# A two-layer encoder on one core: the identity made on GpSimd, x at the head of ScalarE's DMA ring

## The chip, the cores and the metric

The kernel runs on one core of a Trainium2 chip. A core has five engines that run their own instruction queues side by side: TensorE (PE in the profile, with its weight loads as PEld), VectorE (DVE), ScalarE (ACT), GpSimd (POOL) and SyncE (SP). SyncE and ScalarE each issue DMA transfers into a ring of their own; sixteen DMA engines serve both. The metric is the device time of one execution in microseconds, the median of several runs. The kernel before took 605.46 us (604.07 to 605.92 in 3 runs).

## The reference

Two layers over one sequence of 256 tokens, width 1024. Each layer has a mixer with three kinds of attention heads beside each other, and a gated feed-forward part with a short convolution over the tokens:

```python
def mixer_sublayer(x, n1, w_in_l, qg, kg, rpb_l, og, w_out_l, tables):
    h = rms_norm(x, n1)
    proj = h @ w_in_l                       # 1024 -> 2560, cut into q, k, v of three groups
    ...
    out_a = neighbourhood_attention(qa, ka, heads(va, H_NA), rpb_l, na_idx, na_dr, na_dc)
    out_d = dilated_window_attention(qd, kd, heads(vd, H_DIL), dil_idx, dil_val)
    out_c = gqa_block_attention(qc, kc, heads(vc, H_GKV))
    mix = jnp.concatenate([rms_norm(out_a, og[:NA_W]), rms_norm(out_d, ...), rms_norm(out_c, ...)], axis=-1)
    return x + mix @ w_out_l

def channel_sublayer(x, n2, w_gu, cw, cb, w_dn):
    h = rms_norm(x, n2)
    g, u = jnp.split(h @ w_gu, 2, axis=-1)
    g = depthwise_conv_centred(g, cw, cb)
    return x + (jax.nn.gelu(g, approximate=False) * u) @ w_dn
```

For the opening only the first two lines matter: the norm of x and its product with `w_in`.

## The kernel before

**Numbers in two parts.** All large products are done in fp32r, with each operand cut into a high and a low part, and three products per tile: high by high, high by low, low by high (`mm3`). The weights come as raw fp32 in units of up to 1 MB, in four buffers (`wp_raw`); `split` casts each 128x384 or 128x512 piece to the high part on ScalarE (CAST `wp_hi`) and subtracts on VectorE for the low part (TENSOR_TENSOR `wp_lo`).

**The opening.** x is kept on chip as `xs` (`const_x` in the profile): two tiles of 128 tokens by 1024 columns, read as eight column blocks of 128. Its transpose is wanted for the first product. For each block, two 128x128 transposes go through TensorE with the identity `ident` as the moving side (`psw_w<-const_ident,const_x`); ScalarE then scales the result by the norm weight and rounds it to the high part (ACTIVATE `act_hT`), and VectorE makes the low part (SCALAR_TENSOR_TENSOR `act_hT`). This is `split_T`. The norm weights themselves arrive as 16 rows of 128 and are transposed with the same identity (`gains_T`, `psw_w<-const_ident,act_s2k`) before the first ACTIVATE can scale with them. The sums of squares for the norm (`mean_squares`, ACTIVATE `act_s2k<-const_x`, 128x512) run on ScalarE in between; their result enters only later, as a factor on rows.

The first projection, `dq`, is 384 wide: its weights are unit 0 (k blocks 0 to 3, loaded in four pieces) and unit 1 (k blocks 4 to 7, in two). Each unit gives 24 products of 128x384, for two tiles of tokens, four k blocks and three parts.

**Warm-ups.** Before any data is there, TensorE runs products of a constant tile (`const_warm`, filled by GpSimd) into a buffer that nobody reads: `WARM` of them at once, and `WARM_MORE` at a low priority, which the planner puts into holes.

**What sets the order.** Nothing is issued as the Python code runs. `Plan` records every operation with its inputs and outputs, estimates a duration (`cost`), and `Plan.order` then simulates the engines and picks, each time, the operation that can start first; ties go to the lower rank. Rank is the operation's number in the record plus `later` shifts plus an entry of `PLACES`, a long table of small corrections by operation number. `LANDS` tells the planner when each of the first loads is to be expected, in ns. Each engine then runs its list strictly in that order, so an instruction that waits holds up all that stands behind it on its engine.

The first loads stand in a list of their own, `START`: which queue issues what, in which order. `("act", "x", (0, 1))` means that ScalarE's queue loads one block of x, the 0th; "w" is a piece of unit 0, "g" a group of norm weights, "ident" the identity from a constant in memory. These loads are emitted ahead of every other DMA. Eight completion semaphores are used in turn, so the ninth transfer can be issued only when the first has landed, and so on.

Of the kernel before, what the change touches and what calls it, by code (L numbers as in the profile page):

```python
# [18 lines left out]
P = 128  # L19
# [28 lines left out]


START = [  # L50
    ("act", "g", 0), ("sync", "w", 0), ("act", "ident", 0), ("act", "x", (0, 1)), ("sync", "w", 1),
    ("sync", "x", (1, 1)), ("sync", "x", (2, 2)), ("sync", "w", 2), ("sync", "w", 3), ("sync", "x", (4, 2)),
    ("sync", "x", (6, 2)), ("sync", "g", 1), ("sync", "g", 2),
]


LANDS = (3000, 3700, 3200, 3800, 4700, 5000, 6000, 6700, 7300, 8300, 9300, 9350, 9400)


WARM, WARM_MORE, WARM_W = 13, 6, 256  # L60

SUM_ACT, SCALE_ACT = ("dq", "dk", "cq"), ("dk",)

# [166 lines left out]
def handover(a, b):  # L230
# [1 line left out]


PLACES = {
# [35 lines left out]
}  # L270


# [244 lines left out]
def cost(engine, method, args, kw, ins):  # L517

    out = args[0]
    if method == "dma_start":  # L520
        w = out if isinstance(out, View) else args[1]
        small = min(out.shape[-1], args[1].shape[-1]) < 128
        spread = isinstance(args[1], bass.AP) and args[1].ap[0][0] == 0
        stored = isinstance(out, View) and out.tile.pool.dram
        size = 4 * math.prod(w.shape) * (2 if small or spread else 1.5 if stored else 1)
        return 620 if engine == "POOL" else 480, 0, size, None
    n = out.width()
    psum = any(v.tile.pool.psum for v in ins)
    if engine == "PE":
        if method == "transpose":  # L530
            return n / 2.25 + 2.5, 0, 0, "turn"
        n = args[2].width()
        ns = {512: 231.6, 384: 174.5, 256: 118.0}.get(n, n / 2.25 + 2.5)
        if args[1].dtype == mybir.dt.bfloat16:
            ns = 213.0
        if args[1].width() < P:
            return 216.0, 0, 0, "side"
        return ns, 0, 0, "half" if args[1].shape[0] < P else "full"
    if engine == "ACT":
        extra = 88 * sum(isinstance(kw.get(k), View) for k in ("scale", "bias")) + 92 * ("accum_out" in kw)  # L540
        ns = 0.833 * n + (53 if psum else 95) + extra
        return ns, ns + (15 if "accum_out" in kw else 105), 0, None
    if engine == "DVE":
        if method in ("reduce_sum", "reduce_max"):
            n = args[1].width()
        ns = 1.04 * n + (126 if method == "scalar_tensor_tensor" else 68)
        return ns, ns + 82, 0, None
    if method == "memset":
        ns = 190 + 0.83 * n
    elif method == "tensor_copy":  # L550
        ns = 0.92 * n + 100
    elif kw.get("op") == ALU.pow:
        ns = 560 + 150 * n
    elif method == "tensor_scalar":
        ns = 350 + 3.8 * n
    else:
        ns = 830 if out.width() == S else 350 + 3.1 * n
    return ns, ns - 95, 0, None
# [3 lines left out]
def encoder_kernel(  # L562
# [57 lines left out]

    warm = const.tile([P, P], mybir.dt.bfloat16, tag="warm", name="warm")
    nc.gpsimd.memset(warm, 1.0)
    wps = psa.tile([P, WARM_W], F32, tag="a", name="wps")

    def warmed(n):
# [59 lines left out]
    def load(i):  # L685
# [13 lines left out]
        if i == 0:  # L699
            for by, what, c in START:  # L700
                by = nc.scalar if by == "act" else nc.sync
                if what == "w":
                    by.dma_start(rv[:, c], v[:, c])
                elif what == "x":
                    load_x(*c, by)
                elif what == "ident":
                    by.dma_start(ident, c_ident)
                elif what == "g":
                    by.dma_start(gl0 if c == 0 else gl1[16 * c - 16 : 16 * c], gsrc[c])
            nc.first_loads = len(nc.ops)  # L710
        else:
            for c in range(0, a, 2 if i == 1 else a):
                e = c + 2 if i == 1 else a
                nc.sync.dma_start(rv[:, c:e], v[:, c:e])
# [870 lines left out]
```

## Time and profile before

| | |
|---|---|
| median of 3 runs | 605.46 us (604.07 to 605.92) |
| the profiled execution | 605.0 us |
| its span | 603.0 us |
| PE busy | 595.2 us (99%) |
| ScalarE, VectorE, GpSimd busy | 413.3, 471.1, 78.0 us |
| DMA | 121.43 MB, mean 201 GB/s |

The span counts from the first to the last instruction on the core; the 2.0 us around it belong to the execution. The busy time of TensorE includes matmuls whose ends are modelled, so two that overlap in the pipeline show longer than their spacing. In timelines, a name such as `psa_a<-wp_hi,act_hT` is the tile written and the tiles read, without buffer numbers. Nearly all instructions carry one source line, L514, since the planner emits them there; so groups are told apart by tiles and shapes.

### The profile page before, as it was taken

The numbers are of one execution on the slowest core, as the hardware profiler recorded it, in microseconds if no ns is written. First come the engines' busy times: TensorE is split into PE (matmuls) and PEld (weight loads), VectorE is DVE, ScalarE is ACT, GpSimd is POOL, SyncE is SP. The second block draws the span as 40 slices with busy tenths as digits, with TensorE's granted clock in tenths as the row PEclk, the third lists the DMA queues.
The fourth block names the chain that finished last, engine by engine and source line by source line (L and its number), as shares of the span: only waits on it lengthen the run. The fifth ranks groups of instructions, "written<-read, shape, count | busy, mean of one in ns | idle before, by whom it ended". The sixth has DMA issues, their size and how long they took to land.

```text
span 603.0 us, 9676 instructions
## 1 busy us (share of the span) xinstructions
PE 595.2 (99%) x3423; PEld 511.5 (85%) x3423; DVE 471.1 (78%) x983; ACT 413.3 (69%) x1035; POOL 78.0 (13%) x124
## 2 busy tenths in 40 slices
PE   7999999999999999999999999999999999999997
PEld 6998787788888888888899988778888888888886
DVE  2788989897779797987977897668976677767875
ACT  4798989586575685756777898676765555646651
POOL 0652140160000000000014213421000000000000
PEclk9999999999999999999999999999999999999999
DMA  8896323555679898988635826944465455745511
GB/s 276 264 230 193 106 88 109 193 186 181 225 222 281 255 365 298 345 312 275 218 107 173 277 74 245 304 154 139 147 203 174 165 161 199 254 164 193 162 65 71
DMA packets 85216, 121.43 MB, mean 201 GB/s; under 512 B 9880, under 2 KB 69880, under 8 KB 85168
## 3 DMA queue, kind: packets, MB, share of 16 engines
q1 hardware_dynamic: 82992, 112.22, 57.2%
q0 software_dynamic: 1728, 8.39, 4.0%
q8 instruction: 27, 0.44, 0.3%
q10 hardware_dynamic: 448, 0.20, 0.1%
q14 instruction: 21, 0.17, 0.1%
HBM read 110.93 MB, written 9.88 MB: 200 GB/s over the span
## 4 chain that ended last, share of the span: by engine, by line
PE 92%; DMA 3%; DVE 2%; ACT 1%; issue 0%; POOL 0%; ACTq 0%; SPq 0%; DVEq 0%
PE psw_w L514 50%; PE psa_a L514 42%; DMA act_nab<-dram_scr 2%; DMA const_x<-in_x_dram 1%; DMA dram_scr<-act_nab 1%; DVE wp_lo L514 1%; ACT act_s2k L514 0%; DVE act_z L514 0%; DVE act_nab L514 0%; POOL small_rstd L514 0%; ACT wp_hi L514 0%; DVE act_sw L514 0%; ACT act_hT L514 0%; ACTq L514 0%; DVE act_s2k L514 0%
## 5 line engine op out<-in xcount | busy, mean ns | idle before, releaser
L514 DVE TENSOR_TENSOR wp_lo<-wp_raw,wp_hi 128x512 fp32r<-128x512 f32 (+2 forms) x332 | 233.8, 736 | 34.8 <-ACT wp_hi L514 19.3
L514 ACT CAST wp_hi<-wp_raw 128x512 fp32r<-128x512 f32 (+2 forms) x332 | 202.3, 666 | 19.0 <-PE psw_w L514 10.8
L514 PE MATMUL psw_w<-act_hT,wp_hi 128*128 128x512 f32 x704 | 182.8, 393 | 0.0
L514 PEld LDWEIGHTS psw_w<-act_hT,wp_hi 128*128 128x128 f32 x704 | 128.3, 188 | 23.9
L514 PE MATMUL psa_a<-wp_hi,act_hT 128*128 128x384 f32 (+2 forms) x448 | 114.6, 336 | 0.6 <-ACT wp_hi L514 0.6
L514 PEld LDWEIGHTS psw_w<-act_hT,wp_lo 128*128 128x128 f32 x704 | 100.2, 190 | 8.2
L514 PE MATMUL psw_w<-act_hT,wp_lo 128*128 128x256 f32 x704 | 105.2, 282 | 0.0
L514 PEld LDWEIGHTS psa_a<-wp_hi,act_hT 128*128 128x128 f32 x448 | 79.4, 191 | 3.8 <-ACT wp_hi L514 0.7
L514 PE MATMUL psa_a<-wp_lo,act_hT 128*128 128x384 f32 (+2 forms) x224 | 75.3, 338 | 0.0
L514 ACT COPY act_s2k<-psw_w 128x256 f32<-128x256 f32 x88 | 31.7, 372 | 57.5 <-PE psw_w L514 57.1
L514 DVE TENSOR_TENSOR act_s2k<-psw_w,act_s2k 128x256 f32<-128x256 f32 x88 | 36.1, 421 | 42.4 <-ACT act_s2k L514 41.9
L514 PE MATMUL psa_a<-wp_lo,act_ch 128*128 128x512 f32 (+1 forms) x176 | 68.6, 392 | 0.0
L514 PE MATMUL psa_a<-wp_hi,act_cl 128*128 128x512 f32 (+1 forms) x176 | 67.9, 392 | 0.0
L514 PE MATMUL psa_a<-wp_hi,act_ch 128*128 128x512 f32 (+1 forms) x176 | 65.9, 393 | 0.0
L514 PEld LDWEIGHTS psa_a<-wp_lo,act_hT 128*128 128x128 f32 x224 | 42.8, 191 | 2.3 <-DVE wp_lo L514 1.0
L514 PEld LDWEIGHTS psa_a<-wp_hi,act_cl 128*128 128x128 f32 x176 | 33.0, 188 | 7.0
L514 PEld LDWEIGHTS psa_a<-wp_lo,act_ch 128*128 128x128 f32 x176 | 32.9, 188 | 6.6
L514 PEld LDWEIGHTS psa_a<-wp_hi,act_ch 128*128 128x128 f32 x176 | 32.9, 188 | 6.6
L514 DVE SCALAR_TENSOR_TENSOR act_s2k<-act_s2k,act_cw,act_s2k 128x255 f32<-128x255 f32 x88 | 37.1, 478 | 0.0
L514 ACT ACTIVATE act_s2k<-act_s2k 128x512 f32<-128x512 f32 x22 | 13.9, 632 | 31.4 <-DVE act_s2k L514 31.4
L514 ACT ACTIVATE act_s2k<-act_s2k,act_cw 128x256 f32<-128x256 f32 x44 | 24.1, 596 | 14.9 <-DVE act_s2k L514 14.8
L514 POOL TENSOR_TENSOR small_rstd<-small_ms,const_mh 128x6 f32<-128x6 f32 (+2 forms) x26 | 31.3, 1204 | 15.8 <-DVE small_ms L514 14.1
(129 smaller groups left out, 710.7 us busy)
## 6 DMA issues: line engine op xcount, KB each, us to landing
wp_raw<-in_w_gate_up_dram SPq DMA_DIRECT2D x44, 1024.0 KB, 5.2
wp_raw<-in_w_down_dram SPq DMA_DIRECT2D x22, 1024.0 KB, 5.4
wp_raw<-in_w_in_dram SPq DMA_DIRECT2D x14, 768.0 KB, 4.6
wp_raw<-in_w_in_dram SPq DMA_DIRECT2D x8, 1024.0 KB, 5.4
wp_raw<-in_w_out_dram SPq DMA_DIRECT2D x8, 768.0 KB, 6.5
dram_khi<-act_mixT_hi SPq DMA_DIRECT2D x4, 768.0 KB, 5.0
dram_klo<-act_mixT_lo SPq DMA_DIRECT2D x4, 768.0 KB, 8.3
wp_lo<-dram_klo POOLq DMA_DIRECT2D x4, 768.0 KB, 5.7
```

The source lines that it names most:

```text
L514: getattr(o.engine.real, o.method)(*map(real, o.args), **{k: real(v) for k, v in o.kw.items()})
```

## The change

Four things are edited.

1. The identity is no longer loaded. GpSimd fills it with zeros and writes ones where row and column are equal, right behind the fill of the warm-up tile.
2. The list of first loads: ScalarE's ring now carries block 0 and block 1 of x, and nothing else. The norm weights move to second place on SyncE's ring, behind the first weight piece; block 1 of x leaves that ring.
3. `LANDS` follows the new list, `WARM` goes from 13 to 14, and `cost` knows the new GpSimd operation.
4. `PLACES` is a new table, since operation numbers move.

```diff
 START = [
-    ("act", "g", 0), ("sync", "w", 0), ("act", "ident", 0), ("act", "x", (0, 1)), ("sync", "w", 1),
-    ("sync", "x", (1, 1)), ("sync", "x", (2, 2)), ("sync", "w", 2), ("sync", "w", 3), ("sync", "x", (4, 2)),
-    ("sync", "x", (6, 2)), ("sync", "g", 1), ("sync", "g", 2),
+    ("act", "x", (0, 1)), ("sync", "w", 0), ("act", "x", (1, 1)), ("sync", "g", 0), ("sync", "w", 1),
+    ("sync", "x", (2, 2)), ("sync", "w", 2), ("sync", "w", 3), ("sync", "x", (4, 2)), ("sync", "x", (6, 2)),
+    ("sync", "g", 1), ("sync", "g", 2),
 ]
-LANDS = (3000, 3700, 3200, 3800, 4700, 5000, 6000, 6700, 7300, 8300, 9300, 9350, 9400)
-WARM, WARM_MORE, WARM_W = 13, 6, 256
+LANDS = (3400, 3500, 4000, 3600, 5000, 6000, 6800, 7400, 8100, 8900, 8950, 9000)
+WARM, WARM_MORE, WARM_W = 14, 6, 256
...
 PLACES = {
-    76: -86, 77: -11, 80: -43, 82: -43, 112: -35, 123: 210, 150: 217, 155: -22, 156: -22, 159: -329, 174: 52,
+    40: 94, 60: -9, 127: -3, 129: -5, 151: 348, 161: -236, 180: 82, 191: -272, 193: 107, 195: 81, 236: 39, 258: -19,
...
     if method == "memset":
         ns = 190 + 0.83 * n
+    elif method == "affine_select":
+        ns = 900
...
     nc.gpsimd.memset(warm, 1.0)
+    nc.gpsimd.memset(ident, 0.0)
+    nc.gpsimd.affine_select(ident, ident, [[-1, P]], ALU.not_equal, 1.0, base=0, channel_multiplier=1)
...
                 elif what == "x":
                     load_x(*c, by)
-                elif what == "ident":
-                    by.dma_start(ident, c_ident)
```

ScalarE's queue at the start of the program, before (`act_s2k_79` are the norm weights, `const_x` is x, `psw_w` the transposed x in PSUM):

```order
L514 DMA act_s2k_79<-in_norm_g_dram 16x128
L514 DMA const_ident_88<-in_c_ident_dram 128x128
L514 DMA const_x_93<-in_x_dram 128x2x128
L514 ACT_TABLE_LOAD
L514 CAST wp_hi_113<-wp_raw_81 128x384
L514 ACTIVATE act_hT_127<-psw_w_118,const_gains_116 128x256
L514 CAST wp_hi_113<-wp_raw_81 128x384
L514 ACTIVATE act_hT_127<-psw_w_133,const_gains_116 128x256
L514 ACTIVATE act_s2k_150,small_ssx_149<-const_x_93 128x512
L514 ACTIVATE act_s2k_160,small_ssx_149<-const_x_93 128x512
```

And now:

```order
L511 DMA const_x_79<-in_x_dram 128x2x128 x2
L511 ACT_TABLE_LOAD
L511 CAST wp_hi_113<-wp_raw_81 128x384
L511 ACTIVATE act_hT_133<-psw_w_119,const_gains_130 128x256
L511 ACTIVATE act_hT_133<-psw_w_124,const_gains_130 128x256
L511 CAST wp_hi_113<-wp_raw_81 128x384
L511 ACTIVATE act_s2k_154,small_ssx_153<-const_x_79 128x512
L511 ACTIVATE act_s2k_163,small_ssx_153<-const_x_79 128x512
```

Two blocks of x head the queue, and the second hT piece stands ahead of the second cast.

TensorE's queue before, from the last of the 13 first warm-ups on (of the warm-ups only the matmul rows' first and the places between are shown; `act_s2k_79` are the norm weights):

```order
L514 MATMUL psw_w_109<-const_ident_88,act_s2k_79 128x16
L514 LDWEIGHTS const_warm_77
L514 MATMUL psa_a_83<-const_warm_77 128x256
...
L514 MATMUL psw_w_118<-const_ident_88,const_x_93 128x128 x2
...
L514 MATMUL psw_w_133<-const_ident_88,const_x_93 128x128 x2
L514 MATMUL psa_a_139<-wp_hi_113,act_hT_127 128x384
```

And now, behind 15 warm-ups:

```order
L511 MATMUL psw_w_116<-const_ident_85,act_s2k_89 128x16
L511 MATMUL psw_w_119<-const_ident_85,const_x_79 128x128 x2
L511 MATMUL psw_w_124<-const_ident_85,const_x_79 128x128 x2
L511 LDWEIGHTS const_warm_77
L511 MATMUL psa_a_83<-const_warm_77 128x256
...
L511 MATMUL psa_a_143<-wp_hi_113,act_hT_133 128x384
```

Before, two warm-ups stood between the norm weights' transpose and the first of x, and four between the first and second pair of x. Now the three transposes follow each other, and five warm-ups stand between them and the first product.

GpSimd's queue now (before, the fill of `const_mh` followed that of `const_warm` directly, and there was no `const_ident`):

```order
L511 MEMSET const_warm_77 128x128
L511 MEMSET const_ident_85 128x128
L511 ISA
L511 AFFINE_SELECT const_ident_85<-const_ident_85 128x128
L511 MEMSET const_mh_101 128x32
L511 TENSOR_TENSOR small_s1x_230<-small_ssx_153 128x2
```

The ISA row is a configuration of the engine that stood before `small_s1x` and now stands before the select.

65 rows, old and new, of the table PLACES are left out of this document.

## The prediction

> **What bounds the kernel now.** I read the busy times first, then the same in stages, then TensorE's waits, then the opening in order of time. The first line of the page names the engine:
>
> ```profile
> PE 595.2 (99%) x3423; PEld 511.5 (85%) x3423; DVE 471.1 (78%) x983; ACT 413.3 (69%) x1035; POOL 78.0 (13%) x124
> ```
>
> TensorE (PE) has work in 595.2 of 603.0 us. A share over the whole run hides where the other 7.8 us lie, so the next view cuts the span (columns: stretch, its length, then busy time of PE, weight loads, DVE, ACT, POOL, granted clock, DMA share, GB/s):
>
> ```profile
> 0.00:7.00 7.00, 3.80 (x17) 2.15 (x17) 0.65 (x2) 1.79 (x2) 0.46 (x6) 1.00 0.61 181
> 7.00:17.00 10.00, 9.43 (x46) 8.64 (x46) 5.14 (x13) 7.38 (x21) 0.30 (x2) 1.00 1.01 347
> 17.00:100.00 83.00, 82.51 (x564) 72.72 (x566) 72.36 (x205) 72.85 (x258) 30.85 (x45) 1.00 0.54 160
> 100.00:300.00 200.00, 200.00 (x1071) 169.87 (x1068) 167.35 (x291) 134.03 (x258) 14.03 (x25) 1.00 0.78 256
> 300.00:590.00 290.00, 290.00 (x1682) 250.19 (x1681) 218.90 (x465) 195.65 (x498) 32.34 (x47) 1.00 0.53 176
> ```
>
> From 17 to 590 us TensorE lacks half a microsecond. So whatever brings the start of that dense stretch forward brings the end forward by as much, and a change in the opening is worth exactly the shift of the first product of the second weight unit (unit 1). In the timeline of the opening that product is the last row here (start, duration, engine, operation, tiles, count, idle time before and its releaser):
>
> ```profile
> 0.98 2.95 PE L514 MATMUL psa_a<-const_warm 128*128 128x256 bf16 x13 [0.98 <-POOL const_mh L514]
> 4.24 0.26 PE L514 MATMUL psw_w<-const_ident,act_s2k 16*128 16x16 f32 x1 [0.30 <-DMA const_ident<-in_c_ident_dram]
> 6.95 0.69 PE L514 MATMUL psw_w<-const_ident,const_x 128*128 128x128 f32 x2 [1.92 <-DMA const_x<-in_x_dram]
> 7.43 1.06 PE L514 MATMUL psa_a<-const_warm 128*128 128x256 bf16 x4
> 9.36 0.84 PE L514 MATMUL psa_a<-wp_hi,act_hT 128*128 128x384 f32 x2
> 12.75 0.34 PE L514 MATMUL psa_a<-wp_lo,act_hT 128*128 128x384 f32 x1
> 15.21 0.68 PE L514 MATMUL psa_a<-wp_hi,act_hT 128*128 128x384 f32 x3
> 16.98 0.62 PE L514 MATMUL psa_a<-wp_hi,act_hT 128*128 128x384 f32 x2 [0.57 <-ACT wp_hi L514]
> ```
>
> Three things stand there. x arrives only at 6.95: the 13 warm-ups and the gains transpose are long done. Second, a 128x384 product takes 0.52 us at 9.36 (two in 0.84, so 0.32 from start to start), but 0.34 at 12.75 and three in 0.68 at 15.21 (0.17 each): the array runs at half speed up to 12.7. The granted clock in the windows (1.00) doesn't show it; the spacing does. Third, unit 1 waits at the end for ScalarE (ACT), not for data. ScalarE's rows of the same stretch:
>
> ```profile
> 3.43 0.51 ACT L514 CAST wp_hi<-wp_raw 128x384 fp32r<-128x384 f32 x1
> 7.68 0.47 ACT L514 ACTIVATE act_hT<-psw_w,const_gains 128x256 fp32r<-128x256 f32 x1 [3.73 <-PE psw_w L514]
> 8.05 0.50 ACT L514 CAST wp_hi<-wp_raw 128x384 fp32r<-128x384 f32 x1
> 8.96 0.48 ACT L514 ACTIVATE act_hT<-psw_w,const_gains 128x256 fp32r<-128x256 f32 x1 [0.41 <-PE psw_w L514]
> 9.33 0.62 ACT L514 ACTIVATE act_s2k<-const_x 128x512 f32<-128x512 f32 x1
> 13.74 0.84 ACT L514 ACTIVATE act_hT<-psw_w,const_gains 128x256 fp32r<-128x256 f32 x2 [1.54 <-PE psw_w L514]
> 16.41 0.93 ACT L514 CAST wp_hi<-wp_raw 128x384 fp32r<-128x384 f32 x2
> ```
>
> From the first hT at 7.68 to the first cast of unit 1 at 16.41 are 8.73 us, with 0.41 and 1.54 of waiting for TensorE's slow transposes: 6.78 us of ScalarE's own work, eight hT pieces, three casts, four sums of squares.
>
> **The change part by part.** *x.* How long x takes now, and the nearest rows (issue to landing in us, last number; the first row is from the chain of waits, with start and length):
>
> ```profile
> 1.64 5.26 DMA const_x<-in_x_dram
> wp_raw<-in_w_in_dram SPq DMA_DIRECT2D x2, 192.0 KB, 2.8
> const_x<-in_x_dram SPq DMA_DIRECT2D x1, 128.0 KB, 5.1
> const_x<-in_x_dram SPq DMA_DIRECT2D x1, 256.0 KB, 5.6
> 9.42 0.46 SPq L514 DMA_DIRECT2D const_rot<-in_c_rot_dram  x1
> 10.10 0.35 SPq L514 DMA_DIRECT2D const_gq<-in_q_norm_g_dram  x1
> ```
>
> Block 0 is third in its ring now and lands at 6.9. The weight pieces at the head of SyncE's ring need at most 2.8. At the head of ScalarE's ring, issued at 0.72, block 0 lands between 3.5 (2.8) and 6.0 (5.26); I take 3.6, since its rank now is that of the weights. Block 1 follows about 0.45 later (1.17): between 4.0 and 6.4; I take 4.6, since it comes behind twice the bytes. Blocks 2 and 3 keep their slot on SyncE (issued about 2.1, landing now 7.7): at most 7.7, at least 6.3 if all before them flows like the weights; I take 7.2, the old time less 64 KB of identity that is no longer fetched and a part of the slow stretch (181 GB/s up to 7 us, 347 after). The later blocks keep their slots too: SyncE's issues of rot and gq wait for the two x transfers of blocks 4 to 7, which so landed by 9.4 and 10.1; I take 9.2 for the first.
>
> *The identity.* ScalarE's transfer of 64 KB and its issue (0.44 us) go; GpSimd gets a memset and a select over 128x128. Its rows:
>
> ```profile
> 0.72 0.20 POOL L514 MEMSET const_warm<- 128x128 bf16 x1 [0.29 <-POOLq L1570]
> L514 POOL TENSOR_TENSOR act_ccq<-const_rot,const_gq 128x128 f32<-128x128 f32 x2 | 1.5, 766 | 0.1
> L514 POOL TENSOR_TENSOR small_rstd<-small_ms,const_mh 128x8 f32<-128x8 f32 x4 | 6.6, 1644 | 0.3
> ```
>
> The memset ends near 1.1. The trace has no select: its cost lies between the memset's 0.20 and the dearest GpSimd instruction, 1.64; I take 0.77, the pass over the same 128x128. The identity is there at 1.9, at the latest 2.8, against 4.2 now. The 15 warm-ups now ahead of the gains transpose hide it: 0.98 + 15 x 0.213 = 4.18 (13 take 2.95 less the 0.2 that the last one drains). Cost: nothing, up to 4.18; past that, each microsecond is a microsecond. minus_half moves behind the select; its first reader comes past 12 us. Nothing else waits on GpSimd's queue there.
>
> *The norm weights* go from ScalarE's ring to second place on SyncE's. Issued at 1.17 like the second weight piece, which needs 2.8, they land at 4.0: under the same warm-ups. They push that second piece one issue back (0.45 us), to about 4.5; it is first needed after two hT pieces. ScalarE issues two transfers, not three, so its table load ends 0.45 earlier; the first cast then waits for the first weight piece, about as now.
>
> *The sum.* Gains transpose 4.18, first x transpose 4.39, first hT 0.73 later as now (6.95 to 7.68): 5.12. hT, hT, cast (0.37 + 0.37 + 0.50) to 6.36. The squares need x to column 511, so 7.2, a wait of 0.84. From there 1.22 (two squares), 0.82 (two casts), 0.83 (two hT) to 10.07, and 2.67 (as 13.74 to 16.41): unit 1's cast at 12.74 against 16.41, its product at 13.3 against 16.98. **3.7 us earlier.** Does TensorE keep up? With the array at full speed, transposes at 7.2 (0.44), seven products (1.21), eight transposes as soon as x lands at 9.2: hT's third pair can start at 9.9, and ScalarE comes for it at 10.07. It does, barely.
>
> So the clock decides too. In this trace the array doubled at 12.7, after 5.7 us of work without a gap since 6.95; the 2.9 us of warm-ups from 0.98 weren't enough before the gap. The new rows run without a gap from 0.98, so by the same 5.7 us it doubles near 6.7, and the sum above holds.
>
> The Trainium skill, "TensorE: Matmul & The Clock Gate", Part 1, says that the gate opens after about 3.4 us of sustained work, judged in a free-running window. By that rule the doubling here comes between 4.4 and 7.8, the sum stays 601.3, and the first rival below would all but fall out; the trace agrees in kind (a gap of 1.9 us, then 5.7).
>
> *After the opening.* Dense work must find its weights. Between 17 and 590 us no wait for weights shows now. Unit 2, issued by 9.3, moves 768 KB, and ScalarE comes for it near 18.1 (fifth cast from 16.41, 0.43 each): a margin of a few us that shrinks by the shift, with SyncE's issue a little earlier too. I cost it at nothing. The rest of the order is drawn anew from a new table, but TensorE's rows there have the same kinds in the same counts and nearly as many changes between transposes and products; I allow 0.5 us either way.
>
> **The rivals.** *The array stays slow through the opening* (a small gap spoils the run of work). For it: 2.9 us of warm-ups failed here. Against it: 5.7 us without a gap did not. Priced from rows at 0.32 and 0.21 per instruction: four products to 7.6, transposes 8.5, seven products 10.7, four of the eight transposes 11.6, third hT pair 11.85 and not 10.07. The gain falls by 1.8 to 1.9.
>
> *x stays late.* The 5.1 to 5.6 of all x transfers may belong to x's short pieces and not to their rank. Block 1 then lands at 1.17 + 5.26 = 6.4; TensorE has a gap again from 4.85, and by the 5.7 us stays slow to 12.1. Transposes 6.4, warm-ups to 7.9, four products 9.2, transposes 10.0, seven products 12.3, eight transposes at full speed, third hT pair 12.9, then 0.84 + 0.61 + 0.72 + 0.61: cast at 15.8. Gain 0.6. Against it: fewer bytes stand ahead. For it: three x transfers of different rank and ring all took 5.1 to 5.6, so it keeps 0.2.
>
> The Trainium skill, "DMA: Bandwidth & Descriptors", "Issuing engines are not separate DMA queues", says that transfers of all issuers share 16 engines and that a second issuer saves only issue time. By it the new ring itself brings nothing, only the rank, and if block 1 shares the engines with all that SyncE issued it would go as in this rival (604.9). The trace doesn't settle it: x's blocks on both rings took about as long (5.26 and 5.1).
>
> *Slower: the identity is late.* Should GpSimd's select be of another kind than its other instructions (a first use that loads code, say), gains, transposes and hT all stand behind it in TensorE's queue. From the identity to unit 1's cast are 12.74 - 4.18 = 8.56 us, so it decides from 16.41 - 8.56 = 7.9 us on, a select of 6.8 us; at 10 us the run is 2 us longer (607). Against it: nothing on GpSimd takes over 1.7, and its first pow shows no such start.
>
> *The shift isn't carried*: weights or the redrawn order give back 2 us or more. Gain 1.7 or less.
>
> **How the numbers follow.** The profiled execution took 605.0 us (span 603.0 and 2.0 around it), 0.46 under the median of 605.46. 605.0 - 3.7 = 601.3, at the median 601.8. Chances: forecast 0.58 (on its own 600.6 to 602.8: x's third transfer at 6.3 or 7.7 gives a gain of 4.6 or 3.2, and 0.5 for the order); slow array 0.11 (603.6); x late 0.20 (604.9); not carried 0.07 (603.8); slower 0.04. The range 600.6 to 604.5 leaves out the slower case, half of the late x and a little below. Within 0.3% (1.8 us) is about what a measurement here can't tell from no change: faster by more takes the forecast, half of the slow array, a third of the late x (where the array doubles early, gain 2.4) and some of the fourth: 0.71. Same 0.25, slower 0.04.
>
> **What would show it.** Right: x's first transpose near 4.4 and no idle row before it; 128x384 products at 0.17 from 6 to 8 us on; ScalarE waiting for x (not for TensorE) once near 6.4; unit 1's first product near 13.3; less than 1 us of idle from there to 590. Wrong: a wait of TensorE for x over 1 us, products at 0.32 past 10 us, a GpSimd select over 3 us, or new waits for raw weights behind 13 us.

## The result, and the profile after

The changed kernel takes 599.57 us (599.48 to 600.55) against 605.29 us (604.07 to 605.92) for the kernel before beside it: a ratio of 0.9912, 95% interval 0.9893 to 0.993. The profiled execution took 599.53 us with a span of 597.4 us (before 605.0 and 603.0), so 5.5 us less where the prediction had 3.7.

The opening came out as worked out. GpSimd's rows in the changed kernel (start, duration, engine, operation):

```profile
0.86 0.20 POOL L511 MEMSET const_ident<- 128x128 f32 x1
1.15 0.29 POOL L511 TENSOR_SCALAR_AFFINE_SELECT const_ident<-const_ident 128x128 f32<-128x128 f32 x1
```

The identity is there at 1.44 us, far ahead of its first use. TensorE's timeline of the opening:

```profile
0.98 3.32 PE L511 MATMUL psa_a<-const_warm 128*128 128x256 bf16 x15 [0.98 <-POOL const_warm L511]
4.32 0.20 PE L511 MATMUL psw_w<-const_ident,act_s2k 16*128 16x16 f32 x1
4.45 0.66 PE L511 MATMUL psw_w<-const_ident,const_x 128*128 128x128 f32 x4
...
7.07 0.66 PE L511 MATMUL psw_w<-const_ident,const_x 128*128 128x128 f32 x4 [0.48 <-DMA const_x<-in_x_dram]
...
7.74 0.33 PE L511 MATMUL psa_a<-wp_lo,act_hT 128*128 128x384 f32 x1
7.91 0.34 PE L511 MATMUL psa_a<-wp_hi,act_hT 128*128 128x384 f32 x1
...
13.14 0.61 PE L511 MATMUL psa_a<-wp_hi,act_hT 128*128 128x384 f32 x2 [0.34 <-ACT wp_hi L511]
```

Four transposes take 0.66 us at 4.45, where two took 0.69 before: the array is at full speed there already, and two products stand 0.17 us apart at 7.74. Unit 1's first product starts at 13.14 (forecast 13.3, before 16.98). Behind the first hT pieces ScalarE waits for x and not for TensorE, as forecast:

```profile
4.93 0.84 ACT L511 ACTIVATE act_hT<-psw_w,const_gains 128x256 fp32r<-128x256 f32 x2 [0.80 <-PE psw_w L511]
7.13 0.63 ACT L511 ACTIVATE act_s2k<-const_x 128x512 f32<-128x512 f32 x1 [0.79 <-DMA const_x<-in_x_dram]
12.56 1.76 ACT L511 CAST wp_hi<-wp_raw 128x384 fp32r<-128x384 f32 x4
```

The windows (stretch, length, busy PE, weight loads, DVE, ACT, POOL, granted clock, DMA share, GB/s):

```profile
0.00:7.00 7.00, 5.59 (x29) 3.65 (x29) 2.08 (x5) 3.15 (x5) 0.90 (x8) 1.00 0.69 185
7.00:17.00 10.00, 9.59 (x54) 8.37 (x55) 6.66 (x15) 8.97 (x31) 1.69 (x4) 1.00 1.05 353
17.00:100.00 83.00, 83.00 (x575) 73.26 (x575) 74.36 (x208) 74.12 (x259) 29.07 (x44) 1.00 0.58 171
```

By these rows TensorE gained 0.49 us of busy time in the third stretch and nothing behind it. That is too little for the missing 1.8. So I lined up the two traces: TensorE's matmuls in order, each counted at its shortest spacing, and the difference of their start times where the same sum of work stands ahead (called the shift below; it resolves about 0.1 us). It is 3.8 us from 14 us of work on, 5.05 at 110, then flat through the whole feed-forward part, and 5.6 behind layer 2's attention, where it grows between some 365 and 410 us. So 1.25 us come in layer 1's attention and 0.6 in layer 2's. The waits of weight loads (PEld), which the prediction left out, show where such time can hide. Before, 17 to 100 us (total, times, longest):

```profile
PEld psw_w L514 <- ACT act_s2k L514: 1.4, 4, 0.6
...
PEld psa_a L514 <- ACT wp_hi L514: 0.7, 1, 0.7
PEld psa_a L514 <- DVE wp_lo L514: 0.7, 2, 0.4
PEld psw_w L514 <- ACT wp_hi L514: 0.6, 2, 0.4
```

After:

```profile
PEld psw_w L511 <- ACT act_s2k L511: 0.7, 3, 0.3
PEld psw_w L511 <- ACT wp_hi L511: 0.4, 1, 0.4
PEld psw_w L511 <- DVE act_s2k L511: 0.4, 1, 0.4
```

All waits of weight loads for another engine there add up to 4.9 us before and 2.2 after. The busy row of PE hides most of them, since a modelled matmul end covers a late weight load. One wait stands out on VectorE, which masks the neighbourhood bias (a table that layer 1's attention adds to its scores). The bias goes through DRAM and back: VectorE copies it, SyncE stores and loads it. Before, and then after:

```profile
31.83 1.23 DVE L514 COPY act_nab<-act_few 28x1984 f32<-28x1984 f32 x1
48.46 1.43 DVE L514 SCALAR_TENSOR_TENSOR act_nab<-act_nab,const_na 128x576 f32<-128x576 f32 x2 [1.71 <-DMA act_nab<-dram_scr]
```

```profile
27.14 1.24 DVE L511 COPY act_nab<-act_few 28x1984 f32<-28x1984 f32 x1
42.80 1.43 DVE L511 SCALAR_TENSOR_TENSOR act_nab<-act_nab,const_na 128x576 f32<-128x576 f32 x2
```

The copy is 4.7 us earlier, not 3.8, and the mask 5.7 us earlier and without a wait. Two theories fit: the redrawn order took waits away, or the earlier start lets such transfers land in time.

### The profile page after: what moved, and what is told of

It is laid out like the page before. It is cut to its first block, busy times and chain, and to the rows that moved or that the text cites. A ratio compares the mean times of both kernels' runs of the same rounds, so it can differ in the third digit from the quotient of the medians.

```text
span 597.4 us, 9676 instructions
## 1 busy us (share of the span) xinstructions
PE 592.0 (99%) x3424; PEld 509.8 (85%) x3424; DVE 471.0 (79%) x983; ACT 412.7 (69%) x1035; POOL 77.1 (13%) x126
## 4 chain that ended last, share of the span: by engine, by line
PE 97%; ACT 1%; DMA 1%; SPq 0%; issue 0%; DVE 0%; ACTq 0%
PE psw_w L511 51%; PE psa_a L511 46%; DMA const_x<-in_x_dram 1%; ACT act_s2k L511 0%; ACT act_hT L511 0%; ACT wp_hi L511 0%; SPq L511 0%; DVE const_x L511 0%; ACTq L511 0%
## 5 line engine op out<-in xcount | busy, mean ns | idle before, releaser
L511 PE MATMUL psa_a<-wp_hi,act_hT 128*128 128x384 f32 (+2 forms) x448 | 112.0, 333 | 0.3 <-ACT wp_hi L511 0.3
L511 PEld LDWEIGHTS psa_a<-wp_hi,act_hT 128*128 128x128 f32 x448 | 77.8, 189 | 3.5 <-DVE act_hT L511 0.5
```

The source lines that it names most:

```text
L511: getattr(o.engine.real, o.method)(*map(real, o.args), **{k: real(v) for k, v in o.kw.items()})
```

## The experiments

To hold everything still but one thing, these kernels (but for the edits named) take the order of all instructions from a list instead of the planner's choice:

```diff
+ORDER = [0, 1, 2, 3, 4, 5, 6,
...
                 for i in r:
+                    if i != ORDER[len(done)]:
+                        continue
                     o = ops[i]
```

With the list that the planner itself had made, the instructions of each engine are the same as without it.

### 1 to 4: the order, and one instruction in it

Run 1 joins the changed kernel's order up to 20 us of its plan with that of before behind it; run 2 is the mirror image (the order of before up to 24 us, that of the change behind it).

> The changed kernel up to 20 us of its plan, and behind that each engine's instructions in the order in which the kernel before has them. The trace of the change gains 3.8 us up to 17 us and 1.8 us more behind it (1.3 by 100 us, 0.6 between 378 and 398 us). If the redrawn order gives these 1.8 us, this run takes about 601.3 us, and TensorE's weight loads wait about 4.9 us between 17 and 100 us as in the kernel before. If the earlier opening itself gives them (because transfers such as the neighbourhood bias now land in time), it takes about 599.5 us and those waits stay near 2.2 us.

> The mirror image: the kernel before up to 24 us of its plan, and behind that the changed kernel's order on each engine. If the redrawn order is worth 1.8 us by itself: about 603.5 us. If it is worth something only behind the earlier opening: 605.3 us or more, with the vector engine still waiting for the neighbourhood bias near 47 us.

Runs 3 and 4 move one instruction: run 3 is run 1 with

```diff
 VectorE:
-TENSOR_TENSOR wp_lo
 COPY act_nab
+TENSOR_TENSOR wp_lo
```

and run 4 is the changed kernel with the reverse of this.

> The first run of this set with one instruction moved: VectorE's copy of the neighbourhood bias stands one weight split earlier, as in the changed kernel. If that copy's place (it starts the round trip through DRAM for which VectorE waited 1.71 us) makes the 0.67 us step at 54 us: 0.6 to 0.7 us less than the first run of this set. If not: the same time as that run.

> The changed kernel with the same copy moved one weight split later on VectorE, as in the kernel before, and nothing else. If the copy's place makes the 0.67 us step: about 600.2 us, with VectorE waiting about 1 us for the neighbourhood bias near 43 us. If the bias has slack in the new order: 599.5 us, and no such wait.

Measured: run 1 602.2 us (601.16 to 602.9), ratio to before 0.9956, interval 0.9939 to 0.9973, which doesn't meet that of the change; run 2 603.23 (600.88 to 604.55), 0.9974, 0.9958 to 0.999; run 3 601.19 (600.26 to 601.64), 0.9938, 0.9922 to 0.9954; run 4 599.92 (599.39 to 600.66). So **the order gives it, not the earlier start**: with the old order behind it the new opening is worth only 2.8 us, and the new order behind the old opening still 1.7. Together these are 4.5 of the 5.7 us (4.8 where the change was timed again, run 13). In run 1 the weight loads' waits for other engines between 17 and 100 us add up to 5.0 us, as before. The old order even gives shift back. In run 1 the shift is 3.3 us after the opening and 2.35 at the end; its VectorE row:

```profile
45.92 1.43 DVE L809 SCALAR_TENSOR_TENSOR act_nab<-act_nab,const_na 128x576 f32<-128x576 f32 x2 [2.48 <-DMA act_nab<-dram_scr]
```

The bias lands 2.5 us earlier than before where the opening is 3.3 earlier, so VectorE waits longer, and TensorE has a hole of 1.25 us at 52. In run 3 the wait is gone:

```profile
27.61 1.24 DVE L809 COPY act_nab<-act_few 28x1984 f32<-28x1984 f32 x1
43.41 1.42 DVE L809 SCALAR_TENSOR_TENSOR act_nab<-act_nab,const_na 128x576 f32<-128x576 f32 x2
```

One instruction moved by one place is worth 1.0 us in the medians here, though the two intervals still overlap; the traces have 1.0 us in layer 1. Run 4 didn't show the 0.6 us in its median (0.35 over the change, and no more than run 13); its trace has a wait of 0.25 us and 0.6 us less shift from layer 1. In run 2 VectorE still waits 1.68 us for the bias, and the profiled execution, at 604.55 the slowest of that kernel, shows only 0.5 us of gain behind the opening. Its 1.7 us stand on the medians alone.

### 5 and 6: the clock by itself

```diff
-WARM, WARM_MORE, WARM_W = 13, 6, 256
+WARM, WARM_MORE, WARM_W = 13, 29, 256
```

in the kernel before (three of the new warm-ups ahead of the gains transpose, twenty behind it), and in the changed kernel

```diff
-WARM, WARM_MORE, WARM_W = 14, 6, 256
+WARM, WARM_MORE, WARM_W = 4, 6, 256
```

> The kernel before with its own order, its own transfers, and 23 more warm-ups: TensorE has work from 0.98 us until x arrives near 6.9 us. Only the array's speed changes, x doesn't. If the doubled clock carries a part of the gain as the prediction's slow-array rival prices it, 128x384 products stand at 0.17 us from 7 us on and unit 1's first product comes 1.8 to 1.9 us earlier (15.1 us): about 603.2 us. If x's time alone makes the opening's gain: no shift, 605.0 us. If the warm-ups are still running when x comes: up to 1 us later than that.

> The changed kernel and its order with 10 warm-ups fewer ahead of the gains transpose: TensorE works from 0.98 to about 2.05 us and then has nothing until 4.3 us; x, identity and norm weights arrive as in the changed kernel. If the array's speed matters, it is still slow when x's blocks come at 4.4 us (128x384 products at 0.32 us up to 8 to 10 us) and unit 1's first product moves from 13.14 to 13.7 to 15.0 us: 600.1 to 601.4 us. If it doesn't, 599.6 us.

In run 5 unit 1's first product is 2.5 us earlier though x comes only 0.15 us earlier, at full speed from the first transposes on:

```profile
6.80 0.41 PE L813 MATMUL psw_w<-const_ident,const_x 128*128 128x128 f32 x2
...
9.72 0.68 PE L813 MATMUL psa_a<-wp_hi,act_hT 128*128 128x384 f32 x3
...
14.48 0.62 PE L813 MATMUL psa_a<-wp_hi,act_hT 128*128 128x384 f32 x2 [0.54 <-ACT wp_hi L813]
```

And in run 6 it is 1.8 us later than in the changed kernel, though x comes at most 0.2 us later:

```profile
4.46 0.25 PE L809 MATMUL psw_w<-const_ident,act_s2k 16*128 16x16 f32 x1 [2.23 <-DMA act_s2k<-in_norm_g_dram]
...
9.40 0.52 PE L809 MATMUL psa_a<-wp_hi,act_hT 128*128 128x384 f32 x1
9.72 0.52 PE L809 MATMUL psa_a<-wp_lo,act_hT 128*128 128x384 f32 x1
...
14.92 0.62 PE L809 MATMUL psa_a<-wp_hi,act_hT 128*128 128x384 f32 x2 [0.56 <-ACT wp_hi L809]
```

So the array's speed is worth about 1.8 to 2.5 us in the opening, against the 3.8 of the change: the prediction's rival had it at 1.8 to 1.9. The medians: run 6 600.97 us (600.46 to 602.19), 1.4 over the change. Run 5 604.89 (602.3 to 605.33): hardly faster than before, although its opening is. Behind it the old order gave back 1.9 us, 0.5 in layer 1 and 1.5 in layer 2. There TensorE waited for kept weights, which were split in layer 1, parked in DRAM (`dram_khi`, `dram_klo`) and loaded back by GpSimd, a third issuer of transfers beside SyncE and ScalarE:

```profile
PE psa_a L813 <- DMA wp_hi<-dram_khi: 1.5, 1, 1.5
```

Run 6 has the new order, and its shift grows from 2.0 to 3.8 behind the opening, by the same 1.8 us as in the changed kernel.

### 7 and 8: the identity and the rings by themselves

Run 7 is the kernel before, its order kept, with

```diff
-    ("act", "g", 0), ("sync", "w", 0), ("act", "ident", 0), ("act", "x", (0, 1)), ("sync", "w", 1),
+    ("act", "g", 0), ("sync", "w", 0), ("act", "x", (0, 1)), ("sync", "w", 1),
...
+    nc.gpsimd.memset(ident, 0.0)
+    nc.gpsimd.affine_select(ident, ident, [[-1, P]], ALU.not_equal, 1.0, base=0, channel_multiplier=1)
```

Run 8 is the changed kernel, its order kept, without the two GpSimd lines and with

```diff
-    ("act", "x", (0, 1)), ("sync", "w", 0), ("act", "x", (1, 1)), ("sync", "g", 0), ("sync", "w", 1),
+    ("act", "x", (0, 1)), ("sync", "w", 0), ("act", "x", (1, 1)), ("act", "ident", 0), ("sync", "g", 0), ("sync", "w", 1),
```

> The kernel before with its own order, and only the identity changed: GpSimd makes it, ScalarE's transfer of it goes, so that x's block 0 stands second in ScalarE's ring and is issued 0.45 us earlier. If x's lateness belongs to its rank: block 0 comes 0.5 to 0.9 us earlier, but block 1 on SyncE's ring stays where it was (6.7 us), and the array stays slow up to 12 us: a shift of 0 to 0.5 us, 604.5 to 605.0 us. If the identity's 64 KB were what delayed x, both blocks come 1 us or more earlier: 603 to 604 us.

> The changed kernel, its rings and its order, but the identity is loaded, third in ScalarE's ring behind both first x blocks (issued near 1.6 us). From the kernel before, where the identity took 2.9 us from its issue, it lands near 4.6 to 5.2 us, so that gains, transposes and the first hT come 0.3 to 0.8 us later than in the changed kernel. ScalarE waited 0.8 us for x's third transfer there, so most of it is hidden: unit 1's first product 13.1 to 13.6 us, 599.6 to 600.1 us. If the identity on GpSimd carries the gain itself: 1 us or more is lost, 600.6 us or more.

In both expectations the first case fell, and the second came nearer: the identity's transfer is what delayed the opening. Run 7's opening is 3.9 us earlier, all of what the whole change gives, with block 1 of x still on SyncE's ring; run 8 loses 2.9 of it, first of all since TensorE waits for the identity:

```profile
13.06 0.62 PE L812 MATMUL psa_a<-wp_hi,act_hT 128*128 128x384 f32 x2 [0.43 <-ACT wp_hi L812]
```

```profile
6.86 0.20 PE L809 MATMUL psw_w<-const_ident,act_s2k 16*128 16x16 f32 x1 [2.49 <-DMA const_ident<-in_c_ident_dram]
...
7.48 1.02 PE L809 MATMUL psa_a<-const_warm 128*128 128x256 bf16 x5
...
16.06 0.61 PE L809 MATMUL psa_a<-wp_hi,act_hT 128*128 128x384 f32 x2 [0.57 <-ACT wp_hi L809]
```

The identity, issued at 1.74, took 5.0 us; as second in the ring of before it took 2.9. Not all of run 8's loss is the wait: behind it the array falls back to half speed, so that five warm-ups take 1.02 us (0.71 in the change) and products stand 0.32 us apart up to 11 us. Windows of one microsecond show where the transfers lose time. Before, then after (last number: GB/s):

```profile
3.00:4.00 1.00, 0.94 (x5) 0.33 (x3) 0.00 (x0) 0.93 (x2) 0.00 (x0) 1.00 0.86 271
4.00:5.00 1.00, 0.76 (x3) 0.30 (x3) 0.47 (x2) 0.00 (x0) 0.00 (x0) 1.00 0.59 148
```

```profile
3.00:4.00 1.00, 1.00 (x7) 0.62 (x5) 0.00 (x0) 0.40 (x2) 0.00 (x0) 1.00 1.26 341
4.00:5.00 1.00, 0.98 (x8) 0.67 (x7) 0.64 (x2) 0.20 (x2) 0.00 (x0) 1.00 0.62 123
```

The transfers slump between 4 and 5 us (in run 8 to 184 GB/s, in run 7 only to 231). In these four traces the first four transfers to be issued land by 4.4 us (run 7: 4.8), and the fifth and sixth, caught in the slump, at 5.4 to 7.0. Before, x's blocks were fifth and sixth; in run 7 they are fourth and fifth, and land at 4.75 and 5.45. So these landings go by how many transfers stand in front, and not by the ring. With the new list the two blocks land still earlier, at 3.99 and 4.37, but this bought the opening nothing: ScalarE has to wait for x's third transfer, which lands at 7.03 there and at 6.94 in run 7. Run 7's time is 602.28 us (600.87 to 604.25) all the same, 3.05 us under before. In the profiled execution, one of its slowest at 603.84, the old order gave back 2.6 us of the 3.9; its chain of waits:

```profile
29.24 4.66 DMA dram_scr<-act_nab
...
34.66 11.36 DMA act_nab<-dram_scr
...
52.42 0.79 PE psw_w L812 x4
```

Before, that load took 9.65 us. The bias lands at 46.0, 2.3 us earlier than before instead of 3.9, VectorE waits 3.26 us and TensorE 2.0. Run 8 took 602.66 us (600.79 to 603.05).

### 9 to 12: the bias, layer 2, and ScalarE's last square

Run 9 is the kernel before with the copy moved as in run 3, run 11 is run 7 with the same move. Run 10 is the changed kernel with the order of before from 290 us of its plan on, so in layer 2 alone. Run 12 is the changed kernel with

```diff
 ScalarE:
-ACTIVATE act_s2k<-const_x 128x512
 CAST wp_hi x2
+ACTIVATE act_s2k<-const_x 128x512
 CAST wp_hi x2
```

> The kernel before, with nothing moved but the copy of the neighbourhood bias on VectorE, one weight split earlier. In its trace VectorE waits 1.71 us for that bias and TensorE has a hole of about 0.6 us near 54 us. If the copy's place makes the hole: about 0.6 us less than before (604.4 to 604.7 us), and VectorE's wait under 0.5 us. If the round trip lands when the queue lets it, whatever the copy does: no change, wait still near 1.7 us.

> The changed kernel up to the end of layer 1 (290 us of its plan), and from there each engine's instructions in the order of the kernel before. If the last part of the gain (0.6 us at 378 to 398 us in the trace) is the redrawn order of layer 2's attention: 600.1 to 600.4 us, with a wait of TensorE or its weight loads for kept weights (khi) near 375 us as in the runs with the order of before. If it comes from the earlier start alone: 599.6 us.

> The run with the identity alone (602.3 us; its opening came 3.9 us earlier, and 2.8 us of that went again by 50 us where VectorE waited 3.26 us for the neighbourhood bias), with the bias's copy moved one weight split earlier on VectorE as well. If that wait is what ate the shift: VectorE's wait falls under 0.5 us, the shift at 100 us is 3.3 us or more, and the run takes 600.5 to 601.3 us. If the transfer is late for another reason: 602.0 to 602.6 us and the wait stays over 2 us.

> The changed kernel with ScalarE's last sum of squares (0.72 us at 11.95) moved behind the first two casts of unit 1. If ScalarE still sets unit 1's first product: it comes 0.3 to 0.35 us earlier (12.8 us instead of 13.14, when TensorE is through with unit 0), and the run takes about 599.2 us, a difference that only the trace can show. If TensorE or the weights set it: no shift.

Run 9: 604.52 us against 605.04, ratio 0.9995 (0.9982 to 1.0009): no difference. VectorE's wait is gone, but the weight split now behind the copy comes late for TensorE (weight loads wait 0.5 us for wp_lo) and loses near 30 us what the bias gains at 54. Run 11: 600.78 (600.67 to 601.34), 1.5 under run 7; the shift is 4.0 after the opening, 4.1 at 110 us, and VectorE doesn't wait. So the same move is worth nothing behind the old opening and 1.0 to 1.5 us behind the new one. Run 10: 600.48 (599.71 to 600.96), 0.9 over the change, with intervals that overlap. In the traces its shift falls by 0.5 in layer 2 where that of the changed kernel grows by 0.6, at this wait:

```profile
PEld psa_a L809 <- DMA wp_hi<-dram_khi: 0.7, 1, 0.7
```

GpSimd's rows show a reason. In run 10, as in the kernel before, a square stands ahead of the load of these weights, and in the changed kernel behind it; the weights land at 381.0 us against 378.8 there:

```profile
373.45 0.73 POOL L809 TENSOR_TENSOR act_sqm<-act_sqm,act_sqm 128x256 f32<-128x256 f32 x1 [0.21 <-ACT act_sqm L809]
374.14 0.57 POOL L809 DMA_DIRECT2D wp_hi<-dram_khi  x1
```

```profile
372.72 0.54 POOL L511 DMA_DIRECT2D wp_hi<-dram_khi  x1
373.26 0.76 POOL L511 TENSOR_TENSOR act_sqm<-act_sqm,act_sqm 128x256 f32<-128x256 f32 x1
```

No run moves this square alone, so its share isn't shown.

Run 12 is a miss for a faster version: 600.01 (599.82 to 600.85). TensorE no longer waits for ScalarE at unit 1, but then 0.2 us for the low part, x's third transfer was 0.26 us later, and VectorE waited 1.74 us for the bias.

### 13 and 14: does that wait come and go?

Run 13 is the changed kernel once more with its own order written out, run 14 has the copy two weight splits earlier still.

> The changed kernel with its own order written out in full (the same instructions in the same places), profiled and timed once more. If the wait for the neighbourhood bias in the run with the moved square belongs to that square: no wait here, 599.5 us. If it comes and goes between executions: the profile may show a wait of 0 to 2 us near 43 us, the opening's shift lies between 3.3 and 3.8 us, and the times spread over 599.3 to 600.9 us.

> The changed kernel with VectorE's copy of the neighbourhood bias two weight splits earlier (about 1 us). If the wait comes and goes because the bias has hardly any slack: no wait in the profile, and a median at or up to 0.4 us below the run above, unless the two splits that now stand behind the copy come late for TensorE, which would cost 0.3 to 0.5 us near 30 us.

Run 13: 600.06 (598.72 to 600.66), no wait for the bias. Its opening is 3.0 us earlier, not 3.8, since x's third transfer came later. ScalarE's row:

```profile
7.90 0.63 ACT L809 ACTIVATE act_s2k<-const_x 128x512 f32<-128x512 f32 x1 [1.36 <-DMA const_x<-in_x_dram]
```

Behind the opening it gains 1.2 in layer 1 and 0.6 in layer 2, like the first trace of the change. Run 14: 600.25 (599.7 to 600.39), opening 4.2, and a wait of 0.28 us although the copy is 1.7 us earlier than in the changed kernel:

```profile
25.41 1.23 DVE L809 COPY act_nab<-act_few 28x1984 f32<-28x1984 f32 x1
42.71 1.43 DVE L809 SCALAR_TENSOR_TENSOR act_nab<-act_nab,const_na 128x576 f32<-128x576 f32 x2 [0.28 <-DMA act_nab<-dram_scr]
```

The copy doesn't set when the bias is stored there: SyncE issues the store at 28.35, and at 28.40 in the changed kernel:

```profile
28.35 0.62 SPq L809 DMA_DIRECT2D dram_scr<-act_nab  x1
```

```profile
28.40 0.36 SPq L511 DMA_DIRECT2D dram_scr<-act_nab  x1
```

Run 12's wait needn't belong to its moved square: run 8, with the change's own order behind its opening, waits 1.55 us for the bias too. No version is clearly faster than the change.

All shifts against the trace of before in one table, in us (opening at 14 us of work, layer 1 up to 110, layer 2 from there to the end). The last column is VectorE's wait for the bias in layer 1, which is 1.71 us before:

| run | opening | layer 1 | layer 2 | whole | wait |
|---|---|---|---|---|---|
| the change; again (13) | 3.8; 3.0 | +1.3; +1.2 | +0.6; +0.6 | 5.6; 4.8 | none |
| 6, new order, slow array | 2.0 | +1.2 | +0.6 | 3.8 | none |
| 10, old order in layer 2 | 3.4 | +1.2 | -0.5 | 4.2 | none |
| 4, new order, copy back | 3.4 | +0.6 | +0.6 | 4.6 | 0.25 |
| 14, new order, copy sooner | 4.2 | +0.6 | +0.7 | 5.5 | 0.28 |
| 8, new order, identity loaded | 0.9 | +0.4 | +0.6 | 1.9 | 1.55 |
| 12, new order, square later | 3.6 | +0.1 | +0.6 | 4.3 | 1.74 |
| 2, new order, old opening | -0.3 | +0.2 | +0.4 | 0.2 | 1.68 |
| 1, old order | 3.3 | -0.7 | -0.2 | 2.4 | 2.48 |
| 5, old order, fast array | 2.5 | -0.5 | -1.5 | 0.6 | 2.17 |
| 7, old order | 3.9 | -2.3 | -0.3 | 1.3 | 3.26 |
| 3, old order, copy moved | 3.6 | +0.3 | -0.2 | 3.8 | none |
| 11, old order, copy moved | 4.0 | +0.1 | -0.3 | 3.8 | none |
| 9, old order and opening, copy moved | -0.1 | 0.0 | 0.0 | -0.1 | none |

Without a wait for the bias the new order gains 1.2 to 1.3 us in layer 1 and the old one at most 0.3; with a wait the new order keeps 0.1 to 0.6 and the old one loses 0.5 to 2.3. In layer 2 the new order gains in every trace, and the old order loses behind every earlier opening. So layer 1's part of the gain is not safe in each execution, and with both orders free of the wait about 1 us of it still belongs to the rest of the order, which no run takes apart.

## Why the prediction was wrong

**The step that failed** is the term for the order: "The rest of the order is drawn anew from a new table ... I allow 0.5 us either way." Behind the new opening the redrawn order is worth 2.6 us (602.2 in run 1 to 599.57, or 2.1 to the 600.06 of run 13). In the traces 1.8 us show as gain over before, 1.2 in layer 1 and 0.6 in layer 2, and the rest is shift that would have been lost. The term rested on the same kinds and counts of TensorE's rows, and on its busy time, which lacked 0.49 us between 17 and 590 us. That is no bound: its weight loads waited 4.9 us for other engines between 17 and 100 us alone.

**The shift carried whole** ("a change in the opening is worth exactly the shift") failed too, with the other sign. In the profiles with the old order 0.9 (run 1) to 2.6 us (run 7) of the shift went again unless the copy was moved, and by run 7's median 0.85; it went at a bias and at kept weights that come back from DRAM and don't move with the opening. The prediction's last rival named this ("weights or the redrawn order give back 2 us or more") and gave it 0.07; with the redrawn order it didn't happen. For the opening without its order the forecast of 601.8 would have been near, for run 1 took 602.2.

**The opening** was right: 3.8 us against 3.7, and 3.0 to 4.2 in the other traces with these loads and warm-ups (runs 1, 3, 4, 10, 12 to 14), so that a hit within 0.1 is partly luck. First x transpose 4.45 (4.39), first hT 4.93 (5.12), x's blocks 2 and 3 at 7.07 (7.2), casts of unit 1 at 12.56 (12.74). The identity's 0.29 us for the select instead of 0.77 changed nothing under the warm-ups; that it cost nothing, with TensorE as the cover, held.

**x** came early for a reason that the prediction had only in part. It chose "its rank now is that of the weights", which held within 0.4 us (blocks 0 and 1 at 3.99 and 4.37, forecast 3.6 and 4.6), but tied the gain to two things at once. Run 7 shows that the identity's transfer alone was what stood in the way, and that the new list brought the opening nothing more. The Trainium skill, "DMA: Bandwidth & Descriptors", "Issuing engines are not separate DMA queues", says that transfers of all issuers run on the same 16 DMA engines, whoever started them; run 7 agrees (opening 3.9 us earlier with block 1 still on SyncE's ring).

**The clock.** The doubling came between 3.9 and 4.45 and not at 6.7. "By the same 5.7 us" was wrong as a rule, since that time isn't fixed (below); in run 5 about 2.8 us of warm-ups were enough, where the prediction held 2.9 to be too few. The sum held all the same, since it needs full speed only at 7.2. The price of the slow array as a rival, 1.8 to 1.9, was near (1.8 in run 6, 2.5 in run 5).

## What to carry to other kernels

Before a stage is called dense, ask for the waits of the weight loads too, and not for TensorE's busy time alone. A shift in the opening is carried only as far as every transfer behind it moves along; look for round trips through DRAM and what waits for them, since an order that just fits one opening can give back most of the gain of a better one. When a change brings a redrawn order, join old and new halves of the two orders: two such runs tell the parts apart.

## What the runs showed of the hardware

The time from the first work to full array speed isn't constant: 2.8 to 2.9 us in run 5 (warm-ups 0.21 us apart up to 3.73, 0.11 from 3.88), 3.0 to 3.5 in the changed kernel (from 0.98; full speed at 4.45), 5.7 before (6.95 to 12.7), and about 6.2 in run 6 (from 4.46; products 0.32 us apart until 10.68, 0.17 behind it). Run 8 shows both directions: after the wait of 2.49 us the four transposes at 6.99 still run at full speed (0.11 us apart), the array falls to half speed between 7.7 and 7.9, when work has already been back for 0.9 us, and doubles again between 11.1 and 11.3. The Trainium skill, "TensorE: Matmul & The Clock Gate", Part 1, has a window of about 3.4 us that runs free of the kernel, and a busy window opens the gate. Run 8's two changes, about 3.4 us apart, agree with it; run 5's 2.8 us are less than one such window, so there a window that work didn't fill from its start was enough.

The slump of the transfers at 4 to 5 us (148, 123 and 184 GB/s before, with the change and in run 8, against 271 to 341 in the microsecond ahead) has no cause that these traces show.

The late bias can be followed one step further. A transfer here lands in sixteen parts. In run 7 the weight load ahead of the bias in SyncE's queue had twelve of its parts in at 37.0 us, fifteen at 38.3 and the last at 41.5; in the changed kernel twelve were in at 36.7 and the last at 37.3. The last part of this load comes 2.2 to 3.4 us behind the fifteenth in runs 1, 5, 7 and 12, and 1.2 and 1.6 us in runs 2 and 8, all of which wait 1.5 us or more for the bias; it comes within 0.4 us in the change and in runs 3, 6, 9, 10, 11 and 13, which don't wait. (Before, with a wait of 1.71, it is 0.5.) So in those six runs one late part goes with the late bias. With the old order all four traces with the copy in its old place wait (before, 1, 5, 7) and the three with the copy moved don't (3, 9, 11); with the new order runs 2, 8 and 12 wait although the copy stands in its earlier place. What makes the part late stays open.
